# A 3x3 convolution with 2x2 max pooling: sharing the middle-row product between two rows

## The chip, the cores and the metric

The kernel runs on one core of one Trainium2 chip. The metric is the device time of one execution in microseconds (us). Each execution also has a "span", from its first to its last instruction; the device time is about 2 us longer (121.97 against 119.9 us in the profiled run of the changed kernel). Engines: PE is TensorE (matrix multiply), ACT is ScalarE, DVE is VectorE, POOL is GpSimd, SP only issues DMAs here. PSUM is the memory that the matmuls of both kernels write, SBUF that of the other tiles. A "hand-off" is the time between an event on one engine and the start of the work on another that waits for it. An execution more than 1.5% above the fastest of its kernel is marked slow and left out of the ratios, but not out of the medians.

A word on what the timelines show: a PE matmul record lasts 0.38 us although the next one starts 0.216 us later: the records overlap. So a PE gap shorter than about 0.16 us (0.38 - 0.216) does not appear as idle time. Where this document speaks of such gaps, they are differences between the start times of the single matmul records of the trace.

## The reference

```python
# x: (16, 64, 64, 64) f32, weight: (128, 64, 3, 3) f32
x_pad = np.pad(x, ((0,0), (0,0), (1,1), (1,1)))
conv[b, co] += weight[co, ci, kh, kw] * x_pad[b, ci, kh:kh+h, kw:kw+w]   # over ci, kh, kw
output[b, c, i, j] = np.max(conv[b, c, 2*i:2*i+2, 2*j:2*j+2])            # (16, 128, 32, 32)
```

## The kernel before

Two images lie side by side on the 128 partitions (64 input channels each). A "tap pass" is one pair of matmuls that run at the same time (both records of a pair start at 60.10 us in the trace of before), one on the upper 64 partitions for the first image, one on the lower 64 for the second. Each 8-row chunk needs 9 passes. ACT copies each PSUM tile to SBUF and DVE takes the two maxima from there. The input is loaded as f32 and cast to bf16 by ACT (upper half) and DVE (lower half).

```python
for p in range(B // 2):
    nc.sync.dma_start(out=xraw_t, in_=xv[:, 0 : H // 2])          # f32, 1 MB
    nc.sync.dma_start(out=xraw_b, in_=xv[:, H // 2 : H])
    # ... zero the two border rows of xpad on gpsimd ...
    nc.scalar.copy(out=xpad[:, 1 : 33, :], in_=xraw_t)            # cast to bf16
    nc.vector.tensor_copy(out=xpad[:, 33 : H + 1, :], in_=xraw_b)
    for c in range(NCHUNK):                                       # 8 chunks of 8 rows
        for i, k in enumerate([1, 4, 0, 3, 6, 2, 5, 8, 7]):       # 9 taps
            # ... mv: the rows moved by kh and kw; oa, ob: columns of pa, pb ...
            nc.tensor.matmul(oa, wk[k][0:CI, :], mv[0:CI], start=st, stop=sp)
            nc.tensor.matmul(ob, wk[k][CI:128, :], mv[CI:128], start=st, stop=sp)
        for half, pt in ((0, pa), (1, pb)):
            nc.scalar.copy(out=sb, in_=pt)                        # PSUM -> SBUF
            nc.vector.tensor_tensor(out=cm, in0=sb[:, :, 0::2], in1=sb[:, :, 1::2], op=max)
            nc.vector.tensor_tensor(out=oacc[...], in0=cm[:, 0::2, :], in1=cm[:, 1::2, :], op=max)
    # ... store oacc (in two halves) ...
```

Of the kernel before, what the change touches and what calls it, by code (L numbers as in the profile page):

```python
# [1 line left out]

# [5 lines left out]


@with_exitstack
def kernel(
    ctx: ExitStack,
    tc: tile.TileContext,
    x: bass.AP,
    weight: bass.AP,
    pool_size: bass.AP,
    out: bass.AP,
):
    nc = tc.nc  # L20
    FP32 = mybir.dt.float32
    BF16 = mybir.dt.bfloat16

    B, CI, H, W = x.shape
    CO, _, K, _ = weight.shape
    assert pool_size == 2
    HP = H + 2
    WP = W + 2
    HO, WO = H // 2, W // 2

    ROWS = 8
    NCHUNK = H // ROWS

    const = ctx.enter_context(tc.tile_pool(name="const", bufs=1))
    wpsum = ctx.enter_context(tc.tile_pool(name="wpsum", bufs=2, space=bass.MemoryType.PSUM))
    psum = ctx.enter_context(tc.tile_pool(name="psum", bufs=3, space=bass.MemoryType.PSUM))
    xraw_pool = ctx.enter_context(tc.tile_pool(name="xraw_pool", bufs=2))
    xpad_pool = ctx.enter_context(tc.tile_pool(name="xpad_pool", bufs=2))
    colmax_pool = ctx.enter_context(tc.tile_pool(name="colmax_pool", bufs=8))
    oacc_pool = ctx.enter_context(tc.tile_pool(name="oacc_pool", bufs=2))  # L40

    ident = const.tile([128, 128], FP32)
    make_identity(nc, ident)

    wraw = const.tile([CO, CI * K * K], FP32)
    nc.sync.dma_start(out=wraw, in_=weight.rearrange("a b c d -> a (b c d)"))  # L46

    wk = []
    for k in range(K * K):
        wdup = const.tile([CO, 2, CI], FP32, name=f"wdup_{k}")  # L50
        src = wraw.rearrange("a (ci k) -> a k ci", k=K * K)[:, k, :]
        nc.vector.tensor_copy(out=wdup[:, 0, :], in_=src)  # L52
        nc.vector.tensor_copy(out=wdup[:, 1, :], in_=src)  # L53
        wp = wpsum.tile([128, 128], FP32, name="wpsum")
        nc.tensor.transpose(wp, wdup.rearrange("a b c -> a (b c)"), ident)  # L55
        wt = const.tile([128, CO], BF16, name=f"wt_{k}")
        nc.scalar.copy(out=wt, in_=wp)  # L57
        wk.append(wt)

    out_v = out.rearrange("b c h w -> c b (h w)")  # L60

    for p in range(B // 2):
        xv = x[2 * p : 2 * p + 2].rearrange("b c h w -> (b c) h w")
        xraw_t = xraw_pool.tile([128, H // 2, W], FP32, name="xraw_t")
        xraw_b = xraw_pool.tile([128, H // 2, W], FP32, name="xraw_b")
        nc.sync.dma_start(out=xraw_t, in_=xv[:, 0 : H // 2])
        nc.sync.dma_start(out=xraw_b, in_=xv[:, H // 2 : H])

        xpad = xpad_pool.tile([128, HP, W], BF16)
        nc.gpsimd.memset(xpad[:, 0, :], 0.0)  # L70
        nc.gpsimd.memset(xpad[:, H + 1, :], 0.0)  # L71
        nc.scalar.copy(out=xpad[:, 1 : 33, :], in_=xraw_t)  # L72
        nc.vector.tensor_copy(out=xpad[:, 33 : H + 1, :], in_=xraw_b)  # L73

        oacc = oacc_pool.tile([128, 2, HO * WO], FP32)

        for c in range(NCHUNK):
            y0 = c * ROWS
            pa = psum.tile([128, ROWS, W], FP32, name="pa")
            pb = psum.tile([128, ROWS, W], FP32, name="pb")  # L80
            korder = [1, 4, 0, 3, 6, 2, 5, 8, 7]
            for i, k in enumerate(korder):
                kh, kw = k // K, k % K
                st = i == 0
                sp = i == K * K - 1
                rows = xpad[:, y0 + kh : y0 + kh + ROWS]
                if kw == 1:
                    mv = rows.rearrange("p a b -> p (a b)")
                    oa, ob = pa, pb
                elif kw == 0:  # L90
                    mv = rows[:, :, 0 : W - 1]
                    oa, ob = pa[:, :, 1:W], pb[:, :, 1:W]
                else:
                    mv = rows[:, :, 1:W]
                    oa, ob = pa[:, :, 0 : W - 1], pb[:, :, 0 : W - 1]
                nc.tensor.matmul(oa, wk[k][0:CI, :], mv[0:CI], start=st, stop=sp)  # L96
                nc.tensor.matmul(ob, wk[k][CI:128, :], mv[CI:128], start=st, stop=sp)  # L97

            for half, pt in ((0, pa), (1, pb)):
                if half == 0 and c == 5:  # L100
                    nc.scalar.dma_start(
                        out=out_v[:, 2 * p : 2 * p + 2, 0 : HO * WO // 2],
                        in_=oacc[:, :, 0 : HO * WO // 2],
                    )
                pv = pt
                sb = colmax_pool.tile([128, ROWS, W], FP32, name=f"sb{half}")
                nc.scalar.copy(out=sb, in_=pv)  # L107
                cm = colmax_pool.tile([128, ROWS, WO], FP32, name=f"cm{half}")
                nc.vector.tensor_tensor(  # L109
                    out=cm, in0=sb[:, :, 0::2], in1=sb[:, :, 1::2],  # L110
                    op=mybir.AluOpType.max,
                )
                nc.vector.tensor_tensor(  # L113
                    out=oacc.rearrange("p b (h w) -> p b h w", h=HO)[
                        :, half, y0 // 2 : y0 // 2 + ROWS // 2, :
                    ],
                    in0=cm[:, 0::2, :],
                    in1=cm[:, 1::2, :],
                    op=mybir.AluOpType.max,
                )  # L120

        nc.scalar.dma_start(
            out=out_v[:, 2 * p : 2 * p + 2, HO * WO // 2 :],
            in_=oacc[:, :, HO * WO // 2 :],
        )


# [1 line left out]
_INS = ['x', 'weight', 'pool_size']  # L129
_OUTS = [((16, 128, 32, 32), 'float32')]  # L130
#: Inputs that are plain numbers.
_NUMBERS = {'pool_size': 2}


# [26 lines left out]
```

## Time and profile before

| | before |
|---|---|
| device time, median of 4 | 147.03 us |
| span of the profiled run | 145.9 us |
| first pass after which all passes start 0.216 us apart | 18.2 us |
| last pass starts | 139.6 us |

The page of the profile gives first the busy time and share of each engine, then the chain of waits followed back from the last instruction, then groups of instructions (busy time, mean ns of one, idle time before them and who ended it).

```profile
span 145.9 us, 3022 instructions
PE 131.7 (90%) x1161; PEld 58.0 (40%) x1161; DVE 95.2 (65%) x282; ACT 86.2 (59%) x146; POOL 8.6 (6%) x22
...
PE 90%; DMA 4%; ACT 2%; DVE 1%; SPq 0%; issue 0%; ACTq 0%
...
L96 PE MATMUL pa<-xpad,wt 64*128 64x504 bf16 (+1 forms) x576 | 127.6, 382 | 0.0
L109 DVE TENSOR_TENSOR cm<-sb 128x256 f32<-128x256 f32 x128 | 53.6, 423 | 35.9 <-ACT sb L107 35.9
L107 ACT COPY sb<-pa 128x512 f32<-128x512 f32 x64 | 37.5, 585 | 46.2 <-PE pb L97 33.0
```

PE is the chain: 90% of the span, no idle time before its main matmuls. ACT and DVE wait for it. The timeline (start, duration, engine, line, operation) gives the pace of a pass:

```profile
60.10 0.38 PE L96 MATMUL pa<-xpad,wt 64*128 64x512 bf16 x1
60.32 0.38 PE L96 MATMUL pa<-xpad,wt 64*128 64x512 bf16 x1
60.53 0.38 PE L96 MATMUL pa<-xpad,wt 64*128 64x504 bf16 x1
```

A pass starts every 0.216 us, with 504 columns as with 512; 576 passes are 124.4 us. The rest is the start and the tail.

```profile
6.89 1.90 ACT L72 CAST xpad<-xraw_t 128x2048 bf16<-128x2048 f32 x1 [4.88 <-DMA xraw_t<-in_x_dram]
8.69 0.42 ACT L57 CAST wt<-wpsum 128x128 bf16<-128x128 f32 x2
9.00 0.69 PE L55 MATMUL wpsum<-ident,wdup 128*128 128x128 f32 x2 [4.18 <-ACT wt L57]
```

ACT waited for the first load and cast it before it made the first copies of the transposed weights. PE stood still for 4.2 us behind that.

### The profile page before, as it was taken

The numbers are of one execution on the slowest core, as the hardware profiler recorded it, in microseconds if no ns is written. First come the engines' busy times: TensorE is split into PE (matmuls) and PEld (weight loads), VectorE is DVE, ScalarE is ACT, GpSimd is POOL, SyncE is SP. The second block draws the span as 40 slices with busy tenths as digits, with TensorE's granted clock in tenths as the row PEclk, the third lists the DMA queues.
The fourth block names the chain that finished last, engine by engine and source line by source line (L and its number), as shares of the span: only waits on it lengthen the run. The fifth ranks groups of instructions, "written<-read, shape, count | busy, mean of one in ns | idle before, by whom it ended". The sixth has DMA issues, their size and how long they took to land.

```text
span 145.9 us, 3022 instructions
## 1 busy us (share of the span) xinstructions
PE 131.7 (90%) x1161; PEld 58.0 (40%) x1161; DVE 95.2 (65%) x282; ACT 86.2 (59%) x146; POOL 8.6 (6%) x22
## 2 busy tenths in 40 slices
PE   0159999999999999999999999999999999999930
PEld 0023344444444444444444444444444444444410
DVE  0630287686768685878679676867686858586770
ACT  3174644578555955597367755695559555463640
POOL 2000000030001200030003000300002000000000
PEclk9999999999999999999999999999999999999997
DMA  5999995308960598139840994030302112030303
GB/s 164 409 427 427 395 332 231 144 2 236 384 247 3 133 344 334 57 63 284 369 152 16 259 408 184 7 146 0 144 4 84 60 67 81 13 131 4 144 0 144
DMA packets 6813, 25.64 MB, mean 176 GB/s; under 512 B 528, under 2 KB 528, under 8 KB 4752
## 3 DMA queue, kind: packets, MB, share of 16 engines
q1 hardware_dynamic: 2448, 17.07, 32.3%
q10 hardware_dynamic: 4352, 8.39, 15.1%
q8 instruction: 9, 0.15, 0.4%
q14 instruction: 4, 0.03, 0.1%
HBM read 17.07 MB, written 8.39 MB: 175 GB/s over the span
## 4 chain that ended last, share of the span: by engine, by line
PE 90%; DMA 4%; ACT 2%; DVE 1%; SPq 0%; issue 0%; ACTq 0%
PE pa L96 86%; DMA xraw_t<-in_x_dram 4%; PE pb L97 2%; PE wpsum L55 2%; ACT xpad L72 1%; DVE cm L109 1%; ACT sb L107 0%; DVE oacc L113 0%; SPq L46 0%; ACT wt L57 0%; ACTq L107 0%
## 5 line engine op out<-in xcount | busy, mean ns | idle before, releaser
L96 PE MATMUL pa<-xpad,wt 64*128 64x504 bf16 (+1 forms) x576 | 127.6, 382 | 0.0
L97 PE MATMUL pb<-xpad,wt 64*128 64x504 bf16 (+1 forms) x576 | 127.6, 382 | 0.0
L96 PEld LDWEIGHTS <-wt 64*128 64x128 bf16 x576 | 54.8, 95 | 70.5 <-issue 3.6
L109 DVE TENSOR_TENSOR cm<-sb 128x256 f32<-128x256 f32 x128 | 53.6, 423 | 35.9 <-ACT sb L107 35.9
L107 ACT COPY sb<-pa 128x512 f32<-128x512 f32 x64 | 37.5, 585 | 46.2 <-PE pb L97 33.0
L97 PEld LDWEIGHTS <-wt 64*128 64x128 bf16 x576 | 54.8, 95 | 0.5 <-issue 0.5
L113 DVE TENSOR_TENSOR oacc<-cm 128x128 f32<-128x128 f32 x128 | 36.8, 292 | 3.9
L107 ACT COPY sb<-pb 128x512 f32<-128x512 f32 x64 | 37.9, 592 | 0.0
L72 ACT CAST xpad<-xraw_t 128x2048 bf16<-128x2048 f32 x8 | 15.3, 1909 | 4.9 <-DMA xraw_t<-in_x_dram 4.9
L70 POOL MEMSET xpad<- 128x64 bf16 x8 | 7.5, 937 | 101.2 <-DVE oacc L113 101.2
L73 DVE CAST xpad<-xraw_b 128x2048 bf16<-128x2048 f32 x8 | 9.8, 1226 | 3.4 <-DMA xraw_b<-in_x_dram 3.4
L55 PE MATMUL wpsum<-ident,wdup 128*128 128x128 f32 x9 | 3.5, 452 | 8.3 <-ACT wt L57 4.2
L71 POOL MEMSET xpad<- 128x64 bf16 x8 | 7.3, 918 | 0.0
L55 PEld LDWEIGHTS wpsum<-ident,wdup 128*128 128x128 f32 x9 | 1.6, 187 | 10.4 <-ACT wt L57 6.2
L52 DVE COPY wdup<-wraw 128x64 f32<-128x64 f32 x9 | 1.9, 209 | 3.7 <-DMA wraw<-in_weight_dram 3.7
L57 ACT CAST wt<-wpsum 128x128 bf16<-128x128 f32 x9 | 2.2, 265 | 3.1 <-PE wpsum L55 3.1
L53 DVE COPY wdup<-wraw 128x64 f32<-128x64 f32 x9 | 1.9, 208 | 0.0
L72 ACT ACT_TABLE_LOAD x1 | 1.3, 1283 | 0.7 <-PEq L142 0.7
masks.py:199 POOL TENSOR_SCALAR_AFFINE_SELECT ident<-ident 128x128 f32<-128x128 f32 x1 | 0.3, 292 | 0.0
masks.py:197 POOL MEMSET ident<- 128x128 f32 x1 | 0.2, 204 | 0.3 <-POOLq L142 0.3
L142 POOL MEMSET const-float32-0.0<- 128x1 f32 x1 | 0.1, 98 | 0.2 <-issue 0.2
L142 POOL MEMSET const-bfloat16-1.0<- 128x1 bf16 x1 | 0.1, 101 | 0.0
(2 smaller groups left out, 0.2 us busy)
## 6 DMA issues: line engine op xcount, KB each, us to landing
xraw_t<-in_x_dram SPq DMA_DIRECT2D x8, 1024.0 KB, 8.5
xraw_b<-in_x_dram SPq DMA_DIRECT2D x8, 1024.0 KB, 7.0
out_dram<-oacc ACTq DMA_DIRECT2D x16, 512.0 KB, 3.1
wraw<-in_weight_dram SPq DMA_DIRECT2D x1, 288.0 KB, 2.9
```

Of the source, the lines that this page charges most:

```text
L52: nc.vector.tensor_copy(out=wdup[:, 0, :], in_=src)
L55: nc.tensor.transpose(wp, wdup.rearrange("a b c -> a (b c)"), ident)
L57: nc.scalar.copy(out=wt, in_=wp)
L70: nc.gpsimd.memset(xpad[:, 0, :], 0.0)
L71: nc.gpsimd.memset(xpad[:, H + 1, :], 0.0)
L72: nc.scalar.copy(out=xpad[:, 1 : 33, :], in_=xraw_t)
L73: nc.vector.tensor_copy(out=xpad[:, 33 : H + 1, :], in_=xraw_b)
L96: nc.tensor.matmul(oa, wk[k][0:CI, :], mv[0:CI], start=st, stop=sp)
L97: nc.tensor.matmul(ob, wk[k][CI:128, :], mv[CI:128], start=st, stop=sp)
L107: nc.scalar.copy(out=sb, in_=pv)
L109: nc.vector.tensor_tensor(out=cm, in0=sb[:, :, 0::2], in1=sb[:, :, 1::2], op=mybir.AluOpType.max,)
L113: nc.vector.tensor_tensor(out=oacc.rearrange("p b (h w) -> p b h w", h=HO)[:, half, y0 // 2 : y0 // 2 + ROWS // 2, :], in0=cm[:, 0::2, :], ...
```

## The change

The two rows of a pooled row pair are y0 = w0 x[-1] + w1 x[0] + w2 x[1] and y1 = w0 x[0] + w1 x[1] + w2 x[2] (each w a row of three taps). With S = x[0] + x[1]:

- y0 = w1 S + (w2 - w1) x[1] + w0 x[-1]
- y1 = w1 S + (w0 - w1) x[0] + w2 x[2]

The product w1 S ("C", 3 passes) is made once, in y0's PSUM tile, and ACT copies it into y1's PSUM tile (the "seed"); PE then adds 6 passes to y0 ("A") and 6 to y1 ("B"). The seeds are not zero. A group of 16 rows takes 15 passes instead of 18. Loads are cast to bf16 by the DMA (issued by POOL), so the casts on ACT and DVE go. DVE takes the row maximum straight from y1's PSUM tile against y0's evacuated copy. The order of instructions on each engine is the order of the program (on ACT in the loop of after: evacuation at 61.76 us, seed at 62.35, evacuation at 63.26).

```diff
-        nc.sync.dma_start(out=xraw_t, in_=xv[:, 0 : H // 2])
-        nc.scalar.copy(out=xpad[:, 1 : 33, :], in_=xraw_t)       # (and the lower half on DVE)
+            nc.gpsimd.dma_start(out=xb[p][:, a:b, :], in_=xv[:, a:b, :])   # f32 -> bf16
 ...
+    for i in range(8):                    # zeros into both y1 tiles; later matmuls there: start=False
+        nc.tensor.matmul(y1[(i // 2) % 2][:, i % 2], zeros[:, 0:128], zeros, start=True, ...)
 ...
+    def do_c(g): taps(y0[g % 2], G1, <rows of S>, start=True)                  # 3 passes
+    def do_a(g): taps(y0[g % 2], D2, xrows(p, 2*q*R + 1)); taps(y0[g % 2], G0, xrows(p, 2*q*R - 1), ...)
+    def do_b(g): taps(y1[g % 2], D0, xrows(p, 2*q*R));     taps(y1[g % 2], G2, xrows(p, 2*q*R + 2), ...)
+    def seed(g): nc.scalar.copy(out=y1[g % 2], in_=y0[g % 2])                  # PSUM -> PSUM
+    def evac(g, half): nc.scalar.copy(out=ev[g][:, half], in_=y0[g % 2][:, half])
+    def rowmax(g, half): nc.vector.tensor_tensor(out=rm[g][:, half],
+                             in0=y1[g % 2][:, half], in1=ev[g][:, half], op=MAX)
 ...
+    do_s(0); do_c(0); seed(0); do_s(1); do_s(2)
+    for g in range(G):                    # 32 groups of 16 rows
+        # ... load pair g // NQ + 2 ...
+        do_a(g)
+        evac(g, 0)
+        if g + 1 < G:
+            do_c(g + 1)
+            seed(g + 1)
+        do_b(g)
+        evac(g, 1)
+        rowmax(g, 0); rowmax(g, 1)
+        finish(g)                         # column max, store
+        if g + 3 < G: do_s(g + 3)
```

More of the change, by code (lines that the diff above doesn't have):

```diff
@@ L22 @@
     BF16 = mybir.dt.bfloat16
+    MAX = mybir.AluOpType.max
     B, CI, H, W = x.shape
     CO, _, K, _ = weight.shape
-    assert pool_size == 2
-    HP = H + 2
-    WP = W + 2
+    assert pool_size == 2 and K == 3 and CI == 64 and CO == 128
     HO, WO = H // 2, W // 2
-    ROWS = 8
-    NCHUNK = H // ROWS
+    NP = B // 2
+    NQ = 4
+    R = HO // NQ
+    G = NP * NQ
     const = ctx.enter_context(tc.tile_pool(name="const", bufs=1))
-    wpsum = ctx.enter_context(tc.tile_pool(name="wpsum", bufs=2, space=bass.MemoryType.PSUM))
@@ L36 @@
-    psum = ctx.enter_context(tc.tile_pool(name="psum", bufs=3, space=bass.MemoryType.PSUM))
-    xraw_pool = ctx.enter_context(tc.tile_pool(name="xraw_pool", bufs=2))
-    xpad_pool = ctx.enter_context(tc.tile_pool(name="xpad_pool", bufs=2))
-    colmax_pool = ctx.enter_context(tc.tile_pool(name="colmax_pool", bufs=8))
-    oacc_pool = ctx.enter_context(tc.tile_pool(name="oacc_pool", bufs=2))
-    ident = const.tile([128, 128], FP32)
-    make_identity(nc, ident)
+    xb_pool = ctx.enter_context(tc.tile_pool(name="xb_pool", bufs=3))
@@ new lines @@
+    s_pool = ctx.enter_context(tc.tile_pool(name="s_pool", bufs=3))
+    ev_pool = ctx.enter_context(tc.tile_pool(name="ev_pool", bufs=3))
+    rm_pool = ctx.enter_context(tc.tile_pool(name="rm_pool", bufs=3))
+    o_pool = ctx.enter_context(tc.tile_pool(name="o_pool", bufs=4))
+    psum = ctx.enter_context(tc.tile_pool(name="psum", bufs=1, space=bass.MemoryType.PSUM))
+    ctx.enter_context(tc.manual_schedule())
+    y0 = [psum.tile([128, 2, R, W], FP32, name=f"y0_{i}") for i in range(2)]
+    y1 = [psum.tile([128, 2, R, W], FP32, name=f"y1_{i}") for i in range(2)]
@@ L45 @@
     wraw = const.tile([CO, CI * K * K], FP32)
     nc.sync.dma_start(out=wraw, in_=weight.rearrange("a b c d -> a (b c d)"))
-    wk = []
-    for k in range(K * K):
-        wdup = const.tile([CO, 2, CI], FP32, name=f"wdup_{k}")
-        src = wraw.rearrange("a (ci k) -> a k ci", k=K * K)[:, k, :]
-        nc.vector.tensor_copy(out=wdup[:, 0, :], in_=src)
-        nc.vector.tensor_copy(out=wdup[:, 1, :], in_=src)
-        wp = wpsum.tile([128, 128], FP32, name="wpsum")
-        nc.tensor.transpose(wp, wdup.rearrange("a b c -> a (b c)"), ident)
-        wt = const.tile([128, CO], BF16, name=f"wt_{k}")
-        nc.scalar.copy(out=wt, in_=wp)
-        wk.append(wt)
@@ L60 @@
-    out_v = out.rearrange("b c h w -> c b (h w)")
-    for p in range(B // 2):
-        xv = x[2 * p : 2 * p + 2].rearrange("b c h w -> (b c) h w")
-        xraw_t = xraw_pool.tile([128, H // 2, W], FP32, name="xraw_t")
-        xraw_b = xraw_pool.tile([128, H // 2, W], FP32, name="xraw_b")
-        nc.sync.dma_start(out=xraw_t, in_=xv[:, 0 : H // 2])
-        nc.sync.dma_start(out=xraw_b, in_=xv[:, H // 2 : H])
-        xpad = xpad_pool.tile([128, HP, W], BF16)
-        nc.gpsimd.memset(xpad[:, 0, :], 0.0)
-        nc.gpsimd.memset(xpad[:, H + 1, :], 0.0)
-        nc.scalar.copy(out=xpad[:, 1 : 33, :], in_=xraw_t)
-        nc.vector.tensor_copy(out=xpad[:, 33 : H + 1, :], in_=xraw_b)
-        oacc = oacc_pool.tile([128, 2, HO * WO], FP32)
-        for c in range(NCHUNK):
-            y0 = c * ROWS
-            pa = psum.tile([128, ROWS, W], FP32, name="pa")
-            pb = psum.tile([128, ROWS, W], FP32, name="pb")
-            korder = [1, 4, 0, 3, 6, 2, 5, 8, 7]
-            for i, k in enumerate(korder):
-                kh, kw = k // K, k % K
-                st = i == 0
-                sp = i == K * K - 1
-                rows = xpad[:, y0 + kh : y0 + kh + ROWS]
-                if kw == 1:
-                    mv = rows.rearrange("p a b -> p (a b)")
-                    oa, ob = pa, pb
-                elif kw == 0:
-                    mv = rows[:, :, 0 : W - 1]
-                    oa, ob = pa[:, :, 1:W], pb[:, :, 1:W]
-                else:
-                    mv = rows[:, :, 1:W]
-                    oa, ob = pa[:, :, 0 : W - 1], pb[:, :, 0 : W - 1]
-                nc.tensor.matmul(oa, wk[k][0:CI, :], mv[0:CI], start=st, stop=sp)
-                nc.tensor.matmul(ob, wk[k][CI:128, :], mv[CI:128], start=st, stop=sp)
-            for half, pt in ((0, pa), (1, pb)):
-                if half == 0 and c == 5:
-                    nc.scalar.dma_start(
-                        out=out_v[:, 2 * p : 2 * p + 2, 0 : HO * WO // 2],
-                        in_=oacc[:, :, 0 : HO * WO // 2],
-                    )
-                pv = pt
-                sb = colmax_pool.tile([128, ROWS, W], FP32, name=f"sb{half}")
-                nc.scalar.copy(out=sb, in_=pv)
-                cm = colmax_pool.tile([128, ROWS, WO], FP32, name=f"cm{half}")
-                nc.vector.tensor_tensor(
-                    out=cm, in0=sb[:, :, 0::2], in1=sb[:, :, 1::2],
-                    op=mybir.AluOpType.max,
-                )
-                nc.vector.tensor_tensor(
-                    out=oacc.rearrange("p b (h w) -> p b h w", h=HO)[
-                        :, half, y0 // 2 : y0 // 2 + ROWS // 2, :
-                    ],
-                    in0=cm[:, 0::2, :],
-                    in1=cm[:, 1::2, :],
-                    op=mybir.AluOpType.max,
-                )
-        nc.scalar.dma_start(
-            out=out_v[:, 2 * p : 2 * p + 2, HO * WO // 2 :],
-            in_=oacc[:, :, HO * WO // 2 :],
-        )
@@ new lines, with load @@
+    xb, ss = {}, {}
+    def load(p):
+        xv = x[2 * p : 2 * p + 2].rearrange("b c h w -> (b c) h w")
+        xb[p] = xb_pool.tile([128, H, W], BF16, name="xb")
+        ss[p] = s_pool.tile([128, HO, W], BF16, name="s")
+        edges = [0, 18, 40, 64] if p == 0 else [0, 32, 64]
+        for a, b in zip(edges, edges[1:]):
+            nc.gpsimd.dma_start(out=xb[p][:, a:b, :], in_=xv[:, a:b, :])
+    load(0)
+    zeros = const.tile([128, 512], BF16)
+    nc.vector.memset(zeros, 0.0)
+    ident = const.tile([128, 128], BF16)
@@ new lines @@
+    make_identity(nc, ident)
+    for i in range(8):
+        yt = y1[(i // 2) % 2]
+        nc.tensor.matmul(
+            yt[:, i % 2], zeros[:, 0:128], zeros, start=True, stop=True, skip_group_check=True
+        )
+    wv = wraw.rearrange("a (ci k) -> a k ci", k=K * K)
+    wq = const.tile([CO, 16, CI], BF16)
+    nc.vector.tensor_copy(out=wq[:, 1:4, :], in_=wv[:, 3:6, :])
+    nc.vector.tensor_copy(out=wq[:, 4:7, :], in_=wv[:, 0:3, :])
+    nc.scalar.copy(out=wq[:, 0, :], in_=wv[:, 8, :])
@@ new lines @@
+    nc.scalar.copy(out=wq[:, 13:16, :], in_=wv[:, 6:9, :])
+    nc.gpsimd.tensor_sub(out=wq[:, 7:10, :], in0=wv[:, 6:9, :], in1=wv[:, 3:6, :])
+    nc.gpsimd.tensor_sub(out=wq[:, 10:13, :], in0=wv[:, 0:3, :], in1=wv[:, 3:6, :])
+    wt = const.tile([128, 15, CO], BF16)
+    for h, (lo, hi) in enumerate(((0, 8), (8, 15))):
+        tp = y0[1][:, h].rearrange("p a b -> p (a b)").bitcast(BF16)
+        for j in range(lo, hi):
+            nc.tensor.transpose(
+                tp[:, (j - lo) * 128 : (j - lo + 1) * 128],
+                wq[:, j : j + 2, :].rearrange("a b c -> a (b c)"),
+                ident,
+            )
+        src = tp[:, 0 : (hi - lo) * 128]
+        dst = wt[:, lo:hi, :].rearrange("p a b -> p (a b)")
+        if h == 0:
+            nc.vector.tensor_copy(out=dst, in_=src)
+        else:
+            nc.scalar.copy(out=dst, in_=src)
@@ new lines, in wtop, with wbot, taps @@
+    def wtop(m):
+        return wt[0:CI, (m + 1) % 15, :]
+    def wbot(m):
+        return wt[CI:128, m, :]
+    G1, G0, D2, D0, G2 = 0, 3, 6, 9, 12
+    def taps(dst, m0, rows, start=False, skip=None):
+        for kw in (1, 0, 2):
+            i0, i1 = 0, R
+            if skip == 0:
+                i0 = 1
+            if skip == R - 1:
+                i1 = R - 1
+            o0, o1, c0, c1 = (0, W, 0, W) if kw == 1 else (1, W, 0, W - 1) if kw == 0 else (0, W - 1, 1, W)
+            for half, wsel in ((0, wtop), (1, wbot)):
+                lo = half * CI
+                nc.tensor.matmul(
+                    dst[:, half, i0:i1, o0:o1],
+                    wsel(m0 + kw),
+                    rows(lo, i0, i1, c0, c1),
+                    start=start and kw == 1,
+                    stop=True,
+                    skip_group_check=True,
+                )
@@ new lines, in xrows, with get, do_s, do_c @@
+    def xrows(p, first):
+        v = xb[p]
+        def get(lo, i0, i1, c0, c1):
+            a = first + 2 * i0
+            return v[lo : lo + CI, a : first + 2 * (i1 - 1) + 1 : 2, c0:c1]
+        return get
+    def do_s(g):
+        p, q = divmod(g, NQ)
+        v = xb[p]
+        nc.vector.tensor_add(
+            out=ss[p][:, q * R : (q + 1) * R, :],
+            in0=v[:, 2 * q * R : 2 * (q + 1) * R : 2, :],
+            in1=v[:, 2 * q * R + 1 : 2 * (q + 1) * R : 2, :],
+        )
+    def do_c(g):
+        p, q = divmod(g, NQ)
+        st = ss[p]
+        taps(
+            y0[g % 2], G1,
+            lambda lo, i0, i1, c0, c1: st[lo : lo + CI, q * R + i0 : q * R + i1, c0:c1],
+            start=True,
+        )
@@ new lines, in do_a, with do_b, seed, evac @@
+    def do_a(g):
+        p, q = divmod(g, NQ)
+        taps(y0[g % 2], D2, xrows(p, 2 * q * R + 1))
+        taps(y0[g % 2], G0, xrows(p, 2 * q * R - 1), skip=0 if q == 0 else None)
+    def do_b(g):
+        p, q = divmod(g, NQ)
+        taps(y1[g % 2], D0, xrows(p, 2 * q * R))
+        taps(y1[g % 2], G2, xrows(p, 2 * q * R + 2), skip=R - 1 if q == NQ - 1 else None)
+    def seed(g):
+        nc.scalar.copy(out=y1[g % 2], in_=y0[g % 2])
+    ev, rm = {}, {}
+    def evac(g, half):
+        if half == 0:
+            ev[g] = ev_pool.tile([128, 2, R, W], FP32, name="ev")
+        nc.scalar.copy(out=ev[g][:, half], in_=y0[g % 2][:, half])
@@ new lines, in rowmax, with finish @@
+    def rowmax(g, half):
+        if half == 0:
+            rm[g] = rm_pool.tile([128, 2, R, W], FP32, name="rm")
+        nc.vector.tensor_tensor(
+            out=rm[g][:, half], in0=y1[g % 2][:, half], in1=ev[g][:, half], op=MAX
+        )
+    def finish(g):
+        p, q = divmod(g, NQ)
+        o = o_pool.tile([128, 2, R, WO], FP32, name="o")
+        r = rm[g]
+        nc.vector.tensor_tensor(
+            out=o, in0=r[:, :, :, 0::2], in1=r[:, :, :, 1::2], op=MAX
+        )
+        nc.sync.dma_start(
+            out=out[2 * p : 2 * p + 2, :, q * R : (q + 1) * R, :].rearrange(
+                "b c h w -> c b (h w)"
+            ),
+            in_=o.rearrange("p b h w -> p b (h w)"),
+        )
+        del rm[g], ev[g]
@@ L129 @@
+    load(1)
+    do_s(0)
+    do_c(0)
+    seed(0)
+    do_s(1)
+    do_s(2)
+    for g in range(G):
+        if g % NQ == 0 and g // NQ + 2 < NP:
+            load(g // NQ + 2)
+        do_a(g)
[5 more added lines that the diff above has]
+        evac(g, 1)
+        rowmax(g, 0)
+        rowmax(g, 1)
+        finish(g)
+        if g + 3 < G:
+            do_s(g + 3)
 _INS = ['x', 'weight', 'pool_size']
```

## The prediction

> **What bounds the kernel now.** TensorE. The page's chain of waits gives PE 90% of the 145.9 us span. In the timeline at 60 to 66 us a tap pass (both half-array matmuls together) starts every 0.216 us, with 504 or 512 columns, and PE never waits. 576 passes x 0.216 = 124.4 us. The rest: about 9 us until matmuls start (weights, the 1 MB load, the 1.9 us cast), cold passes of 0.425 us until 18.0 us, and 6 us after the last matmul (139.9 to 145.9). ACT (59%) and DVE (65%) are off the chain.
>
> **What the change removes.** 15 passes for 18 on each 16-row group: 32 x 15 = 480 passes, 103.7 us, so 20.7 us less PE work, all on the critical path. The casts (ACT 15.3 us, DVE 9.8 us) and POOL memsets also go, but were hidden.
>
> **What it adds.** Per group, ACT makes the seed copy (1024 columns, PSUM to PSUM) and two 512 evacuations. A 512 copy takes 0.588 us; back-to-back copies start 0.49 us apart. [...] before's copies (0.588 us at 512, casts 1.91 us at 2048) give 0.86[...]. So the seed is estimated at 1.02 us, ACT at 1.9 us per group. DVE: two max of 512 from PSUM, one max to 512 outputs, one bf16 add of 512. The slope of before's groups (0.423 us at 256, 0.292 at 128) gives 0.69 us for 512, so about 2.3 to 2.6 us per group. Both stay under PE's 15 x 0.216 = 3.24 us.
>
> **The new critical loop.** In PE order A (6 passes), C (next, 3), B (6), the next A may start only when the seed copy has read C's result, and only B lies between. From the timeline: ACT starts 0.47 us after the start of the last pass it needs; PE starts about 0.16 us after an ACT copy (transposes at 12 us). Loop = 8 x 0.216 + 0.47 + 1.02 + 0.16 = 3.38 us against 3.24. So PE should wait for the seed 0.1 to 0.15 us in each group, some 4 of the 20.7 us given back.
>
> **Sum (estimate).** First A pass at about 10 us (weights at 3.7 us, products, transposes, PSUM copies of 1.2 us, S add, C, seed); 31 x 3.37 + 2.6 = 107; cold clock +1; tail 0.25 + two max 1.4 + one 0.7 + store 2.8 = 5.1. Span about 123; the timed median was 0.85 above the span. **Prediction 124 us, 8 in 10 between 118 and 132; faster by over 2%: 0.94, within 2%: 0.04, slower: 0.02.**
>
> **What the profile would show.** Right: 480 pairs of main matmuls at 0.216 us; 3.3 to 3.4 us per group; PE waiting for ACT's seed about 30 times, 0.1 us each; DVE 70 to 80%, ACT 55 to 65% busy; the last third as fast as the first. Wrong: PE waiting for DVE (row max or S late), for loads, or not at all (3.24 per group, 120 us).
>
> **What would make it wrong.** (1) The seed takes longer than 1.02 us: each 0.1 us costs 3 us. (2) Max with a PSUM input is slower than its SBUF slope, and row max holds the next seed. (3) The casting loads from POOL come late. [...] before shows POOL memsets of 0.15 us stretched to 1.2 us beside DVE's cast. [...] loads run two pairs (26 us) ahead, so I expect little. (4) Start: the first 18 rows or the POOL subtractions late.

The 0.86 is in ns per element, from the two copies named beside it.

## The result, and the profile after

The changed kernel took 122.08 us (median of 4, 121.54 to 122.36) against 147.03 us. The ratio is 0.830, 95% interval 0.827 to 0.833; both predicted "faster" and the range 118 to 132 hold. A ratio here is the mean time of one kernel's fast runs over the mean of the other's fast runs of the same rounds, so it is not quite the ratio of the medians.

The page of the changed kernel:

```profile
span 119.9 us, 2463 instructions
PE 110.4 (92%) x983; PEld 57.5 (48%) x983; DVE 76.3 (64%) x132; ACT 69.7 (58%) x100; POOL 11.4 (9%) x25
...
PE 88%; DMA 5%; DVE 2%; issue 1%; ACT 1%; DVEq 0%; POOLq 0%
...
L127 PE MATMUL y<-xb,wt 64*128 64x504 bf16 (+3 forms) x768 | 88.9, 377 | 1.1 <-ACT y L174 1.1
L186 DVE TENSOR_TENSOR rm<-y,ev 128x512 f32<-128x512 f32 x64 | 41.2, 686 | 30.5 <-PE y L127 30.5
L181 ACT COPY ev<-y 128x512 f32<-128x512 f32 x64 | 37.6, 590 | 37.3 <-PE y L127 37.3
L174 ACT COPY y<-y 128x1024 f32<-128x1024 f32 x32 | 31.9, 997 | 1.9 <-PE y L127 1.6
```

PE is still the chain. The seed (L174) takes 0.997 us. PE waited for it visibly once, 1.1 us, at the start; the forecast wait in every group is not there. The timeline of one group in the loop:

```profile
61.48 0.83 PE L127 MATMUL y<-s,wt 64*128 64x512 bf16 x6
61.76 0.58 ACT L181 COPY ev<-y 128x512 f32<-128x512 f32 x1 [1.15 <-PE y L127]
...
62.13 2.66 PE L127 MATMUL y<-xb,wt 64*128 64x512 bf16 x24
62.35 1.00 ACT L174 COPY y<-y 128x1024 f32<-128x1024 f32 x1
...
63.26 0.59 ACT L181 COPY ev<-y 128x512 f32<-128x512 f32 x1
```

C's three passes start at 61.48, B and the next A follow at 62.13, with no break that the timeline shows. The single records say: C's last pass starts at 61.916, the seed 0.43 us later at 62.35; the seed ends at 63.35 and the next A starts at 63.396. This is one of the groups whose B leaves out the zero border row, and there PE did wait, too briefly to show: the last pass of B takes 0.189 us and A starts 0.237 us after it, so 0.05 us. In groups of full length A starts 0.216 us after the last pass of B and 0.08 us after the seed's end: no wait.

To see where the time went, I cut each span in three: up to the first of the last 28 groups' passes (the last 504 passes before, the last 420 after); these passes, called "28 groups", the last one counted as 0.216 us; and the tail behind them.

| us | before them | 28 groups | tail | span |
|---|---|---|---|---|
| before | 30.93 | 108.92 | 6.02 | 145.87 |
| after | 24.23 | 89.90 | 5.76 | 119.89 |
| difference | -6.70 | -19.02 | -0.26 | -25.98 |

28 x 3 x 0.216 is 18.1 us of the loop's 19.0; most of the other 0.9 is that after leaves out the zero border row: 3 passes in each of 14 groups take 0.19 us, not 0.216, which is 1.1 us, less the 0.05 us that PE waits in 7 of them. In the first column, the 4 groups' 12 passes less are 2.6 us, so roughly 4 us came from the start itself, which I had not forecast in that size.

### The profile page after: what moved, and what is told of

Its sections match the earlier page's. It is cut to its first block, busy times and chain, and to the rows that moved or that the text cites. A ratio compares the mean times of both kernels' runs of the same rounds, so it can differ in the third digit from the quotient of the medians.

```text
span 119.9 us, 2463 instructions
## 1 busy us (share of the span) xinstructions
PE 110.4 (92%) x983; PEld 57.5 (48%) x983; DVE 76.3 (64%) x132; ACT 69.7 (58%) x100; POOL 11.4 (9%) x25
## 3 DMA queue, kind: packets, MB, share of 16 engines
q1 hardware_dynamic: 8848, 8.69, 21.7%
## 4 chain that ended last, share of the span: by engine, by line
PE 88%; DMA 5%; DVE 2%; issue 1%; ACT 1%; DVEq 0%; POOLq 0%
PE y L127 88%; DMA xb<-in_x_dram 5%; DVE rm L186 1%; ACT y L174 1%; DVE o L194 1%; DVE s L148 0%; DVEq L186 0%; POOLq L243 0%
## 5 line engine op out<-in xcount | busy, mean ns | idle before, releaser
L127 PE MATMUL y<-xb,wt 64*128 64x504 bf16 (+3 forms) x768 | 88.9, 377 | 1.1 <-ACT y L174 1.1
L127 PEld LDWEIGHTS <-wt 64*128 64x128 bf16 x960 | 54.8, 95 | 52.0 <-issue 4.7
L186 DVE TENSOR_TENSOR rm<-y,ev 128x512 f32<-128x512 f32 x64 | 41.2, 686 | 30.5 <-PE y L127 30.5
L181 ACT COPY ev<-y 128x512 f32<-128x512 f32 x64 | 37.6, 590 | 37.3 <-PE y L127 37.3
L174 ACT COPY y<-y 128x1024 f32<-128x1024 f32 x32 | 31.9, 997 | 1.9 <-PE y L127 1.6
L127 PE MATMUL y<-s,wt 64*128 64x504 bf16 (+1 forms) x192 | 27.3, 386 | 0.8 <-DVE s L148 0.8
L194 DVE TENSOR_TENSOR o<-rm 128x512 f32<-128x512 f32 x32 | 22.2, 694 | 1.1
L148 DVE TENSOR_TENSOR s<-xb 128x512 bf16<-128x512 bf16 x32 | 13.4, 420 | 4.0 <-DMA xb<-in_x_dram 4.0
L67 POOL DMA_DIRECT2D xb<-in_x_dram x17 | 9.2, 547 | 65.8 <-PE y L127 65.0
L79 PE MATMUL y<-zeros 128*128 128x512 bf16 x8 | 3.6, 630 | 1.2 <-DVE zeros L73 1.2
```

The costliest lines, as they stand in the source:

```text
L67: nc.gpsimd.dma_start(out=xb[p][:, a:b, :], in_=xv[:, a:b, :])
L79: nc.tensor.matmul(yt[:, i % 2], zeros[:, 0:128], zeros, start=True, stop=True, skip_group_check=True)
L127: nc.tensor.matmul(dst[:, half, i0:i1, o0:o1], wsel(m0 + kw), rows(lo, i0, i1, c0, c1), start=start and kw == 1, stop=True, skip_group_che ...
L148: nc.vector.tensor_add(out=ss[p][:, q * R : (q + 1) * R, :], in0=v[:, 2 * q * R : 2 * (q + 1) * R : 2, :], in1=v[:, 2 * q * R + 1 : 2 * (q ...
L174: nc.scalar.copy(out=y1[g % 2], in_=y0[g % 2])
L181: nc.scalar.copy(out=ev[g][:, half], in_=y0[g % 2][:, half])
```

## The experiments

My theory after reading the result: the seed loop is not absent, it is as long as PE's own 15 passes, with some 0.03 us to spare. The rival: ACT, 58% busy, simply has room. Further questions: what the sharing alone is worth, what the loads and the max from PSUM are worth, and what decides the start. All runs gave correct results. Times of "28 groups" are cut as in the table above, so differences of the start do not enter them.

### Evacuations in front of the seed

```diff
         do_a(g)
         evac(g, 0)
+        evac(g, 1)
 ...
         do_b(g)
-        evac(g, 1)
```

> Both evacuation copies of y0 are put in front of the seed on ACT instead of one on each side; no engine gets more work. Theory (the seed loop is as long as PE's own 15 passes, with about 0.03 us to spare per group, read from PE's start-to-start gaps around the shortened edge groups): in the trace of after the seed starts at 62.35, 0.44 us after the start of C's last pass; with a second copy in front it can start only about 0.49 us after the second copy's start, near 62.74. That is 0.39 later, less 0.03 to spare: PE waits about 0.36 us in some 30 groups, +9 to +11 us, span 129 to 131, time about 132. Rival (ACT is busy 58% only, so it has room and the order does not matter): span 119.9 +- 0.5.

Measured: 130.81 us (ratio 0.892, 0.886 to 0.897), span 128.7, just under the expected range, 28 groups in 98.82 us instead of 89.90. No engine has more work, only the order on ACT differs. ACT's timeline in this run:

```profile
61.85 1.07 ACT L181 COPY ev<-y 128x512 f32<-128x512 f32 x2 [1.56 <-PE y L127]
62.81 1.03 ACT L174 COPY y<-y 128x1024 f32<-128x1024 f32 x1
```

C's last pass started at 62.07 here, so the seed came 0.74 us after it instead of 0.43, and took 1.03 us. The next A started at 63.896, 0.31 us later than PE could have. The rival falls.

### A small dose in front of the seed

```diff
     def seed(g):
+        nc.scalar.copy(out=sc, in_=y0[g % 2][:, 1, 0:2, :])   # 128 columns, thrown away
         nc.scalar.copy(out=y1[g % 2], in_=y0[g % 2])
```

> A small dose in the loop: ACT copies 128 columns of C's result to a scratch tile directly in front of each seed. Such a copy took 0.27 us, and two in a row started about 0.16 us apart, so the seed is delayed by about 0.16 us. Theory (0.03 us to spare): PE waits 0.13 us per group, +4 us, span near 124. This is the size of the wait that I had forecast and that the changed kernel does not show. Rival (there is real slack of 0.1 us or more in the loop, PE's queue hides the hand-off): less than 2 us.

Measured: 128.53 us (ratio 0.875, 0.871 to 0.879), span 126.3, 28 groups in 95.99 us: +6.1 us in the 28 groups, more than the 4 expected. The dose was larger than I thought: the scratch copy itself started 0.49 us after C's last pass, the seed another 0.16 later, and the seed took 1.02 us, together 0.24 us of delay. PE waited 0.206 us in a group of full length.

### Sharing undone

```diff
-            y0[g % 2], G1, <rows of S>, start=True,                 # C from S
+            y0[g % 2], G1, xrows(p, 2 * q * R), start=True,         # C from x[0] alone
-        taps(y0[g % 2], D2, ...)
+        taps(y0[g % 2], G2, ...)
-        taps(y1[g % 2], D0, xrows(p, 2 * q * R))
+        taps(y1[g % 2], G1, xrows(p, 2 * q * R + 1), start=True); taps(y1[g % 2], G0, xrows(p, 2 * q * R))
-            seed(g + 1)      # and do_s
```

> The changed kernel with 18 passes again: no sum S, no seed copy, y1 computed directly; loads, evacuation, max, start and tail as in the changed kernel. Theory (the gain is PE passes on the critical path): 96 passes x 0.216 = 20.7 us more in the loop, no seed wait at the start (about 1 us less): span 139 to 141, time about 142; so sharing explains about 20 of the 26 us of span and the rest is start and tail. Rival (a good part comes from casting loads, the shorter DVE and ACT work or better scheduling of the loop): span under 136.

Measured: 139.15 us (ratio 0.948, 0.941 to 0.955), span 137.7, a little under the expected range. The 28 groups took 107.75 us: 17.85 more than after, which is 20.4 for all 32 groups, as expected. But the part before them took 24.20 us, the same as after's 24.23, although it holds 12 passes more. So sharing loses about 2.6 us at the start between these two executions: the sum S and the first seed are latency that nothing hides (PE waited 0.81 and 1.08 us for them in after), and PE's clock, of which more below, was full from 10.1 us here and only from 13.4 us in after. This run does not separate the two. Against the kernel before, 8.2 us of span (7.7 us between the medians of time) come from the rest of the change.

### Casting loads alone, in the kernel before

```diff
-        nc.sync.dma_start(out=xraw_t, in_=xv[:, 0 : H // 2])     # and xraw_b
-        nc.scalar.copy(out=xpad[:, 1 : 33, :], in_=xraw_t)       # and DVE's cast
+        nc.gpsimd.dma_start(out=xpad[:, 1 : 33, :], in_=xv[:, 0 : H // 2])
+        nc.gpsimd.dma_start(out=xpad[:, 33 : H + 1, :], in_=xv[:, H // 2 : H])
```

> The kernel before with the casting loads alone (f32 to bf16 on POOL's queue straight into the padded tile, three buffers; the 16 cast instructions go). Theory (casts were hidden behind PE): loop unchanged at 0.216 us per pass, only the start moves, by -1 us (no 1.9 us cast, load lands about 1 us later): span 144.5 to 146. Rival (casts cost time): span under 143.

Measured: 144.34 us (ratio 0.986, 0.979 to 0.992, by the 2% rule unclear), span 141.4: below the theory's range, where the rival had put it. But the loop is as the theory says: 28 groups in 108.92 us, exactly as before. The start gained 4.85 us (26.08 against 30.93), not 1. This is between two single executions, and the one profiled here was this run's fastest: its four spans are 141.4 to 143.4 us, those of before in the same rounds 144.3 to 145.7, so the gain between the medians is 2.7 us of span, 2.5 us of time. The timeline of this run shows where it comes from:

```profile
4.07 2.94 PE L55 MATMUL wpsum<-ident,wdup 128*128 128x128 f32 x7 [4.07 <-POOL xpad L66]
...
4.56 0.48 ACT L57 CAST wt<-wpsum 128x128 bf16<-128x128 f32 x2 [2.54 <-PE wpsum L55]
```

With no cast in front of them, ACT's weight copies start at 4.56 us instead of 8.69 us. I had read the cast as 1.9 us of work; what it cost was, by the two traces, the order: ACT waited for a load with the weight copies behind it. The passes then follow each other from 9.4 us instead of 13.6 us. No run changes the order alone.

### f32 loads and casts back into the loop of after

```diff
+        if p >= 2:      # f32 load on SP's queue into xr[p], two halves
+            return
 ...
         finish(g)
+        if 2 <= pn < NP and g % NQ == 0: nc.scalar.copy(out=xb[pn][:, 0:32, :], in_=xr[pn][0])
+        if 2 <= pn < NP and g % NQ == 2: nc.vector.tensor_copy(out=xb[pn][:, 32:64, :], in_=xr[pn][1])
```

> The casting loads undone inside the loop only (image pairs 2 to 7 load f32 as before and are cast in halves, 1.9 us on ACT and 1.2 us on DVE per pair; pairs 0 and 1 and the start unchanged). Theory (stall = what delays the seed less 0.03 us): the ACT cast starts at once after the second evacuation and runs 0.56 us past the time at which the next first evacuation is due, so the next seed is late by about 0.45 us in 6 groups: +2.5 us, span 122 to 123.5; DVE has 0.8 us of idle time per group, so its cast costs nothing. Rival (casts are hidden as they were in the kernel before, where taking them away left the loop at 0.216 us per pass): span 119.9 +- 0.5.

Measured: 127.95 us (ratio 0.873, 0.867 to 0.878), span 126.7, far above the range. Two things are mixed. The 28 groups took 92.45 us, +2.55 us, the 2.5 expected. The rest, 4.4 us, is a flaw of my edit: the f32 load of pair 2 has nothing to wait for, so it went out at 1.2 us and, as I read it, competed with the first loads: PE waited 4.3 us for the first S, in after 0.8, and C of group 0 started at 11.25 us instead of 8.14; the clock was full for good only from 19.0 us. The verdict on casts rests on the loop alone. ACT's timeline there:

```profile
32.67 1.91 ACT L233 CAST xb<-xr 128x2048 bf16<-128x2048 f32 x1
34.47 0.60 ACT L187 COPY ev<-y 128x512 f32<-128x512 f32 x1
34.95 1.04 ACT L180 COPY y<-y 128x1024 f32<-128x1024 f32 x1
```

PE's timeline at the same place shows the wait as idle time, because it is long enough here:

```profile
36.04 1.26 PE L133 MATMUL y<-xb,wt 64*128 64x512 bf16 x10 [0.25 <-ACT y L180]
```

C's last pass had started at 34.096, so the seed came 0.85 us after it. PE waited 0.43 us in each of six groups, 2.6 us in all. DVE's cast of 1.22 us made no gap. So a cast that was free in the kernel before costs time once the loop is tight.

### Max from SBUF instead of PSUM

```diff
+        nc.scalar.copy(out=ey[g][:, half], in_=y1[g % 2][:, half])
         nc.vector.tensor_tensor(out=rm[g][:, half],
-            in0=y1[g % 2][:, half], in1=ev[g][:, half], op=MAX)
+            in0=ey[g][:, half], in1=ev[g][:, half], op=MAX)
```

> The max straight from PSUM undone: ACT copies y1 to SBUF too (two more 512 copies per group), DVE takes the max of two SBUF tiles. Theory: ACT's two more copies fit between the second evacuation (next start possible at 63.75 in the trace of after) and the next first evacuation (due at 64.97), 0.98 us of work in 1.2 us, so the seed is not delayed; only the tail grows by about 0.6 us: span 120 to 121. Rival (reading PSUM from DVE is a needed part of the gain, ACT goes from 58% to over 80% busy and holds the seed): span over 123.

Measured: 120.39 us in the median (119.92 to 122.62), span 118.2, which is lower than after and than expected. The lines of its page:

```profile
PE 108.8 (92%) x983; PEld 55.9 (47%) x983; DVE 76.3 (65%) x132; ACT 101.1 (86%) x164; POOL 11.4 (10%) x25
...
L189 DVE TENSOR_TENSOR rm<-ey,ev 128x512 f32<-128x512 f32 x64 | 41.4, 688 | 30.1 <-ACT ey L188 30.1
```

ACT rises to 86% and DVE's max takes 688 ns instead of 686, so the operand's place does not matter to DVE here. The 28 groups took 90.67 us, +0.77, and the tail 6.35 us, +0.59: taking the max from PSUM is worth about 1.4 us here. That the seed would not be delayed was wrong by a little: it starts 0.49 us after C's last pass instead of 0.43, although the copy in front of it on ACT had started 0.70 us before, and PE waits 0.02 us in each group of full length. Why this hand-off is longer stays open. That the run is still faster comes from the part before the 28 groups, 21.16 us against 24.23, where the edit only adds work. Two things differ there: the first sum S, which waits for the first load, began at 6.32 us instead of 7.66, and the passes ran at 0.216 us from the first C on, those of after did not. Executions of one kernel can differ in this way: one of this kernel's four (122.62 us, marked slow) is as long as those of after. This led to the next two runs.

### Dummy matmuls at the start

```diff
+    def dummy(n):   # n matmuls of zeros into y1[1], which is not in use yet
         # after each of the two blocks of weight transposes:
+        dummy(2)
 ...
     do_c(0)
+    dummy(3)
     seed(0)
```

> Seven dummy matmuls of zeros put into PE's gaps at the start (2 after each block of transposes, 3 after C of group 0), so PE has no gap over about 0.5 us from 1.2 us on. In after the clock is full only from 13.4 us, 2.7 us after the first A pass. Theory (the gaps at 5.4, 7.1 and 9.4 us keep the clock low): full clock by about 8 us, some 12 passes at 0.216 instead of 0.38 to 0.43 us: span 117.5 to 118.5. Rival (zero operands or the waits for loads decide): 119.9 +- 0.4.

> The kernel with seven dummy matmuls again, in the same rounds as the changed kernel. If the gaps at the start keep the clock low, every execution should have full clock by about 7 us and the median should be 2 to 3 us below the changed kernel's: 119 to 120 us. If its earlier gain was chance[...], the two medians agree within 0.5 us.

> The changed kernel again, unchanged, as the yardstick of the next two in the same rounds. 121.5 to 122.4 us expected. The start depends on when the clock becomes full, which differed by chance between runs (full at 13.4 us in the profiled run of after, at 5.4 us in the profiled run of the y1 evacuation), so single runs may lie up to 3 us lower.

Measured: 119.61 us in the first rounds (ratio 0.817, spans 116.9 to 117.7); in the second, five rounds beside the unchanged after: 119.47 us (0.812, 0.808 to 0.816) against 122.08 us (0.829, 0.826 to 0.833). All 10 executions of the dummy version lay between 119.05 and 120.53 us, all 10 of after between 121.43 and 122.51 us. So it is not chance. First PE's timeline of after at the start, then that of the dummy version in its second job:

```profile
6.42 0.91 PE L96 MATMUL y<-ident,wq 128*128 128x128 bf16 x7 [0.78 <-DVE wt L104]
8.14 1.46 PE L127 MATMUL y<-s,wt 64*128 64x512 bf16 x6 [0.81 <-DVE s L148]
10.69 2.58 PE L127 MATMUL y<-xb,wt 64*128 64x512 bf16 x12 [1.08 <-ACT y L174]
```

```profile
7.58 0.82 PE L134 MATMUL y<-s,wt 64*128 64x512 bf16 x6
8.33 0.82 PE L94 MATMUL y<-zeros 128*128 128x512 bf16 x3
9.49 1.39 PE L134 MATMUL y<-xb,wt 64*128 64x512 bf16 x12 [0.34 <-ACT y L181]
```

The six passes of the first A take 2.58 us in after and 1.39 us with dummies. In after, passes start 0.37 to 0.43 us apart until 13.4 us. A pass takes up to 0.427 us there and 0.216 us later, and the moment of the change differs between executions: in the repeated run of after the transposes already ran at full pace from 4.8 us, but after the gaps that followed, the passes fell back to 0.43 us at 9.9 us and were full again only at 15.1 us. The granted clock, the number behind POOL's busy time, shows when. First two stretches of the repeated run of after, then one of the dummy version in the same job:

```profile
core 0: us, PE busy (x) PEld busy (x) DVE busy (x) ACT busy (x) POOL busy (x), PEclk, DMA share, GB/s
4.70:8.11 3.41, 1.52 (x20) 1.12 (x20) 1.12 (x2) 0.91 (x1) 2.65 (x5) 1.00 1.03 194
8.11:14.94 6.83, 5.75 (x30) 2.33 (x28) 0.85 (x2) 2.76 (x4) 0.00 (x0) 0.50 1.07 215
```

```profile
6.95:10.36 3.41, 3.07 (x25) 1.19 (x25) 0.43 (x2) 1.90 (x2) 0.46 (x1) 1.00 1.08 214
```

In the repeated run of after the clock was full for these 3.41 us, then half for 6.83 us. In the stretch before it fell, PE was busy for 1.52 of the 3.41 us, and the longest distance between two PE starts had been 1.32 us (1.00 and 1.32 us between 5.0 and 7.7 us; a third, 1.75 us, came later). In the first 3.41 us of full clock of the dummy version PE was busy for 3.07, and there it did not fall. The mean granted clock of single executions agrees: it was 0.971 or less in six of the ten executions of after and 0.985 or more in all ten with dummies. In the y1 evacuation, with full clock from 5.9 us by its trace (not from 5.4, as the expectation above has it), PE was busy for 1.75 of the first 3.41 us and the clock did not fall, so what makes it fall was not shown.

The granted-clock figure counts the time before the first clock record as full. It shows the fall above as 0.50, but reads 1.00 for a stretch of after in which passes took up to 0.43 us until 13.4 us, because the trace of after has no clock record before 13.38 us:

```profile
core 0: us, PE busy (x) PEld busy (x) DVE busy (x) ACT busy (x) POOL busy (x), PEclk, DMA share, GB/s
8.14:21.40 13.26, 12.18 (x94) 5.60 (x95) 5.48 (x10) 6.73 (x10) 0.00 (x0) 1.00 0.94 195
```

### Group 0 without sharing

```diff
-    do_s(0); do_c(0); seed(0); do_s(1)
+    taps(y0[0], G1, xrows(0, 0), start=True); do_s(1)
 # in do_a and do_b: for g == 0 the direct taps G2, G0 and G1, G0, G2
```

> Group 0 is computed directly with 18 passes, without sum and seed; groups 1 to 31 share as in after. The run without sharing started its passes at 7.4 us and was at full clock at 10.2 us, against 8.1 (then a wait of 1.1 us for the seed) and 13.4 us in after. Theory (the first seed is latency with nothing to hide it): C of group 1 starts at about 10.8 instead of 13.0 us, A of group 1 at about 13.3 instead of 14.9: span 118 to 118.7. Rival (loads of rows 18 and up limit the start): 119.5 or more.

Measured: executions of 121.42, 118.36, 118.52 and 120.16 us; the profiled one, the longest, had a span of 118.4. The ratio of 0.808 uses only the two marked fast and flatters it; the median of all four is 119.34. In the profiled run A of group 1 starts at 13.7 us instead of 15.2 (expected: 13.3 instead of 14.9), with the clock full at 10.7 us instead of 13.4. So leaving out the first sum and seed helps the start; how much of it is their latency and how much the clock, this run does not separate. I did not combine it with the dummies: with full clock the three extra passes cost 0.65 us, and in the dummy version 1.25 us lie between the end of C and the first A (the dummies fill 0.65 of them), so by estimate 0.6 us could be gained.

### Three more changes at the ends

```diff
+    nc.sync.dma_start(out=xf, in_=<first 18 rows, f32>)      # then cast by ACT and DVE
-        tp = y0[1][:, h]...                                  # PSUM of the transposes
+        tp = y0[1 - h][:, h]...
+        dummy(3 * h)                                         # and dummy(3) after do_c(0)
 # last group: column max and store for each half by itself, on two queues
```

> Dummy matmuls, and three more changes at the ends: the first 18 rows come as f32 on SP's queue and are cast by ACT and DVE (the casting load of them landed at 7.6 us; before's plain load of 32 rows landed at 6.9), the second block of transposes uses another PSUM buffer so that it need not wait for the copy of the first (0.8 us), and the last group's max and store go by halves. Theory: C of group 0 starts at about 6.6 instead of 7.9 us, the tail shrinks by 0.2: 1 to 1.5 us less than the dummy version. Rival (the three loads at the start share the DMA engines, the first rows land no earlier): within 0.5 us of it.

Measured: 118.91 us (0.807, 0.804 to 0.811), 0.6 us less than the dummy version; one of six executions, marked slow, took 124.43 us. The tail fell from 5.75 to 5.37 us, by 0.4 where 0.2 was expected. The start did not move: the first A began at 9.49 us in both. The f32 rows landed at 6.0 us, but their cast took DVE until 6.6, and the copy of the weights, which was ready before, came after it. I traded one wait for another. This version is the fastest that I ran, and beats both kernels.

## Why the prediction was right or wrong

**Right: PE bounds both kernels and the passes are the gain.** Undoing the sharing alone puts 17.85 us back into 28 groups; 28 x 3 x 0.216 is 18.1.

**Right: the casts were hidden, ACT and DVE stay under PE.** The loop of before does not change by 0.01 us without its casts. After shows ACT at 58% (forecast 55 to 65) and DVE at 64%, below the forecast 70 to 80. But that share counts the start and the tail: DVE was busy for 76.3 us in 32 groups, 2.4 us in each, within the forecast 2.3 to 2.6, and for 72% of the time in the loop (66.52 of the 92.60 us from 21.4 to 114.0 us). The max operations took the forecast 0.69 us each (686 and 694 ns).

**Wrong in size: "PE should wait for the seed 0.1 to 0.15 us in each group, some 4 of the 20.7 us given back".** The prediction itself had named no wait, 3.24 us per group and 120 us as a sign that it would be wrong, and that is what came. The loop exists, but its terms were too long. Forecast: 8 x 0.216 + 0.47 + 1.02 + 0.16 = 3.38 us. Measured: 8 x 0.216 + 0.43 + 0.997 + 0.05 = 3.21 us. Most of the error is the hand-off from ACT to PE, which I took from transposes at the start (0.16 us), where it is 0.05 us in the loop. PE needs 3.24 us, so 0.03 us is left. Five delays of different kind agree on that number (delay of the seed's end against after, worked out from the start times and durations quoted above; wait as PE's start-to-start gap less the length of a pass):

| what delays the seed against B's end | delay | PE's wait | difference |
|---|---|---|---|
| after, groups whose B leaves out the border row (3 passes 0.027 shorter) | 0.08 | 0.05 | 0.03 |
| scratch copy in front | 0.24 | 0.21 | 0.03 |
| second evacuation in front | 0.34 | 0.31 | 0.03 |
| ACT cast, f32 loads | 0.46 | 0.43 | 0.03 |
| y1 evacuation (longer hand-off) | 0.056 | 0.022 | 0.03 |

So the kernel sits at the edge: PE and the seed loop differ by 1%.

**Mis-sized, and cancelling: start, tail and the time outside the span.** The first A began at 10.7, not 10 us, and the cold passes, those at 0.37 to 0.43 us, cost more than the 1 us allowed. The effective start (end of the last pass less 477 passes of 0.2141 us) is 12.0 us against the 11 forecast. The tail was 5.76 us, not 5.1. I took the time outside the span as 0.85 us from executions that were not the same; in the same executions it is 2.1 us for after and 1.8 for before. Together: 4.0 less for the wait that is not there, 0.9 less for border rows, 1.0 + 0.7 more for start and tail gives 119.9 of span instead of 123.1; 1.2 more outside it gives 122. That 124 was near is partly luck.

**Not foreseen: the start of the kernel before.** I listed its 9 us but did not ask what they waited for. The casting loads are worth 2.5 us between the medians of time in the kernel before (4.85 us between the two profiled executions), and the sharing then gives back about 2.6 us at the start of the profiled after, part of it through the clock (full from 13.4 us there, from 10.1 us in the run without sharing).

**Loads from POOL came in time.** No wait for a load appears after 11.2 us in after; the prediction's warning that they could come late was not needed. What DVE's work does to POOL's loads no run here tests by itself.

What stays open: why the run with the y1 evacuation had its first load 1.3 us earlier and full clock from the first C on, though nothing at its start was edited, and why three of its four executions were faster than any of after. The clock was full from 5.9 us in that run, from 13.38 us in after, from 4.70 us (and then half again) in the repeated run of after and from 6.95 us in the dummy version of the same job; what sets the moment was not shown. Also open is why the time outside the span is 0.3 us longer in after.

## What to carry to other kernels

When a change cuts the bounding engine's work, write down the new loop that passes through the other engines, term by term, and take each hand-off from the same kind of place in the trace; a share of 58% busy says nothing about such a loop, its order does. Look at what the engine queues wait for in the first 10 us: a wait for a load in front of unrelated work, and gaps on PE that zero matmuls can fill (with the granted clock then 0.985 or more in all ten executions), were worth about 2.5 us each here between medians (146.83 against 144.34 and 122.08 against 119.47 us). Compare runs by stretches of the trace, so that chance at the start is not taken for an effect in the loop.
